# RWKV-7 trunk on one core: the chunk inverse from 16-blocks, its product in 64x64 tiles, and two stages in program order

## The chip, the core and the metric

The kernel runs on one core of a Trainium2 chip. A core has TensorE (PE, which writes its products to PSUM), VectorE (DVE), ScalarE (ACT) and GpSimd (POOL), and SyncE (SP), which issues most transfers. Each engine runs its own list of instructions from front to back; semaphores tie the lists together. The metric is the device time of one execution in microseconds (us).

## The reference, cut to what matters

Two decoder layers on 512 tokens of width 1024. The change lies in the first, the RWKV-7 time mixing. For each of 16 heads of width 64 a state matrix S runs through the tokens:

```python
def step(S, inp):
    r_t, d_t, k_t, v_t, a_t, b_t = inp
    sa = jnp.einsum('bhij,bhj->bhi', S, a_t)
    S = (S * d_t[:, :, None, :] + sa[..., None] * b_t[:, :, None, :]
         + v_t[..., None] * k_t[:, :, None, :])
    return S, jnp.einsum('bhij,bhj->bhi', S, r_t)
...
y = ((y - mean) * lax.rsqrt(var + GN_EPS)).reshape(B, T, D)      # per head
bonus = jnp.sum(r_h * k_h * r_k.astype(f32), axis=-1, keepdims=True) * v_h
y = y + bonus.reshape(B, T, D)
return (y * g.astype(f32)).astype(x.dtype) @ w_o
```

Behind it come a convolutional FFN, the attention layer and a second FFN; nothing in them is changed.

## The kernel before

The tokens are cut into 8 chunks of 64 (`CH`). Within a chunk the recurrence becomes matrix algebra: per chunk and head a unit triangular 64x64 matrix has to be inverted; after that the chunk needs only products, and a scan over the 8 chunks carries the state. Heads stand in pairs: 8 pairs `q`, and `h` = 0 or 1 for the upper or lower 64 partitions.

The stage goes from about 196 to 423 us of the span. First part, the operands:
- `v_steps` makes V with 16 groups of 12 products of 512 columns (L745). For two groups it takes a block of weights, which ACT rounds to fp32r (`whi`, L102) and POOL subtracts (`wlo`, L107); in the first eight groups ACT and DVE also make the mixed input `xv` (L337, L342, L719, L720).
- `inverse(hf)` handles four chunks, `E0` or `E1`. `mats` multiplies `bk` with `ar` into 64x64 matrices (L953) and masks them into `E` (L955). The two 32x32 diagonal blocks of each are then laid out with one matrix per partition by DVE transposes (L964) and inverted by substitution: 30 columns `k`, for each a product into `tmp` (L978) and a sum (L979) over (31-k)*k numbers. Transposes bring the result back (L987, L991); the block off the diagonal takes two rounds of 32x32 products (`corner`, L1001) and copies by ACT (L1004).
- `attn_mats` makes per chunk the matrices `G` (L912) and `R` (L920). Each is masked either by DVE straight from PSUM (L890) or by an ACT copy (L887) and a POOL product (L888).
- `with_inverse` (L933) multiplies `G` of a chunk with its inverse; ACT copies the result out (L936).

Second part, `scan`, per chunk: products of `G` with the state (L1103) and of `ar` with the state (L1106); DVE and ACT copy the solution out (L1110, L1111); a product with `bT` (L1120) gives the new state, which DVE puts together (`sn` L1123, `SV` L1125); `R` ends the output `py` (L1129); `bkT` (L1034) makes the next chunk's `bT`. `norm` of a chunk is called one chunk later: eight small steps on DVE and ACT (L1044 to L1053), after which PE transposes `yc` and `bv` (L1062) and ACT copies them (L1063). From chunk 4 on two output gates follow per chunk (`gate`: ACT L1163, POOL L1164 and L1165, PE L1168, then `gated`: DVE L1180, L1181, ACT L142, DVE L143). In the chunks 0 to 3 `fill` places steps of the second inverse and of `attn_mats` between these.

What sets the order: a string `ORDER` says how the program emits the operands' steps (`V`, `N`, `M`, `s`: one step of V, of `mats`, of `attn_mats`, of the inverse), the tables `FM` and `FS` how many steps `fill` emits. That is only the order of emission. The program is built with a scheduler that models each engine and moves instructions against each other; only a stretch under `tc.manual_schedule()` stays as emitted. Before, that is the projections' stage (string `START`) alone; the operands and the scan are moved by the scheduler.

Of the kernel before, what the change touches and what calls it, by code (L numbers as in the profile page):

```python
# [35 lines left out]
KS = (99, 26)  # L36
# [11 lines left out]
MV = 2  # L48
VLO = 'PPPPDDDD'
VB = (4, 4)  # L50
ORDER = 'VVNVNVNVNVsssMVsMVsMVMVMMsssssVMMsssssVMMsssssVMMnsssssVMMnsssssnMMssssssVsVsnMVVnssVsMb'
SCB = 6
AORD = 'qsqqqsqsqspsqoqspvpsqvspvsvpqspoqsvpvspvqsvovpsopvppvpossovvvpovvppo'
PTB = 2
# [12 lines left out]
CC = {}  # L67
# [9 lines left out]
class Net:  # L77
# [272 lines left out]
    def rwkv(self, after_pool):  # L350
        nc, tc, d, par = self.nc, self.tc, self.d, self.par
# [5 lines left out]
        gm = pA.tile([128, 2, T], F32, name="gm")  # L357
# [3 lines left out]
        cst = pA.tile([128, CC["gmask"]], F32, name="cst2")  # L361
        tri, mask = (cst[:, CC[k]:CC[k] + 128] for k in ("tri", "mask"))
# [9 lines left out]
        eng = {"D": nc.vector, "P": nc.gpsimd}  # L372
# [17 lines left out]
        for k in FIRST:  # L390
            q = nc.scalar if k.isupper() else nc.sync
# [308 lines left out]
        bs, box = self.ps(), {}  # L700
# [50 lines left out]
        v = v_steps()  # L751
        box["m"] = lambda: t2("m")
        sums = lambda: None
        for q in range(8):
# [6 lines left out]
            for n in range(4):  # L761
                ns = slice(n * 128, n * 128 + 128)
# [38 lines left out]
        sp0 = tc.alloc_tile_pool(name="s0", bufs=1, reuse_waits="tile")  # L801
        aa0 = tc.alloc_tile_pool(name="aa0", bufs=1, reuse_waits="tile")
        mixv = tc.alloc_tile_pool(name="rX", bufs=1, reuse_waits="tile")
        box["m"] = lambda: mixv.tile([128, T], F32, name="m", tag="m", bufs=MV)
        self.ar, self.bk, self.fdec, self.amask, self.gmask = ar, bk, fdec, mask, tri

        nc.sync.dma_start(tri, d["cst"][:, CC["gmask"]:CC["gmask"] + 128])

        def bonus():
# [7 lines left out]
            for h in range(2):  # L817
# [3 lines left out]
        E0, n0, s0 = self.inverse(0, sp0, sp0)  # L821
# [1 line left out]
        A0, m0 = self.attn_mats(0, aa0, "A")  # L823
        run = {"M": lambda: next(m0, None), "V": lambda: next(v, None), "N": lambda: next(n0, None), "n": lambda: next(n1, None),
               "s": lambda: s0(1), "S": lambda: s1(1), "b": bonus}
        for k in ORDER:
            run[k]()
        for g in (v, m0, n0, n1):
            for _ in g:
                pass  # L830
        s0(99)
        mixv.release()
        w24.release()
        A1, m1 = self.attn_mats(1, self.mixp, "mx")
        sp = tc.alloc_tile_pool(name="sc", bufs=1, side="right", reuse_waits="tile")
        rest = self.scan(sp, (A0, A1), (E0, E1), m1, s1, aa0, sp0, gm)
        for p in (sp, self.mixp, pB):
            p.release()
        if self.dbg:
# [85 lines left out]

    def with_inverse(self, G, E, n0):

        nc = self.nc
        P = [self.ps().rearrange("a (q x) -> a q x", q=8) for _ in range(2)]
        for q in range(8):  # L930
            for h in range(2):
                hs = slice(64 * h, 64 * h + 64)
                nc.tensor.matmul(P[h][:, q, :], G[hs, q, :], E[hs, n0 + q, :], start=True, stop=True, skip_group_check=True)  # L933
        A = G.rearrange("a q x -> a (q x)").rearrange("a (h q x) -> a h q x", h=2, q=8)
        for h in range(2):
            nc.scalar.copy(A[:, h], P[h])  # L936
        return A

    def inverse(self, hf, pool, sp):

        nc = self.nc
        box = {}
        E = pool.tile([128, 32, CH], F32, name=f"E{hf}", tag=f"E{hf}", bufs=1)

        def mats():
            for c4 in range(4):
                p = self.ps()
                for q in range(8):  # L950
                    for h in range(2):
                        hs = slice(64 * h, 64 * h + 64)
                        nc.tensor.matmul(p[hs, CH * q:CH * q + CH], self.bk[hs, q, 4 * hf + c4, 0, :], self.ar[hs, q, 0, 4 * hf + c4, :],  # L953
                                         start=True, stop=True, skip_group_check=True)
# [4 lines left out]
        def tin(qd):
            if qd == 0:  # L960
                box["P"] = sp.tile([128, 32, 32], F32, name="P", tag="P")
            dd = qd % 2
            rows = slice(32 * qd, 32 * qd + 32)
            nc.vector.transpose(box["P"][rows], E[rows, :, 32 * dd:32 * dd + 32].rearrange("a n t -> a t n"))  # L964

        def nin(h):
            if h == 0:
                box["NT"] = sp.tile([128, 32, 32], F32, name="NT", tag="NT")
            nc.vector.transpose(box["NT"][64 * h + 32:64 * h + 64], E[64 * h:64 * h + 32, :, 32:64])

        def sub(k):
            n, P = 31 - k, box["P"]
            eng = nc.gpsimd if k > KS[hf] else nc.vector
            tmp = sp.tile([128, 256], F32, name="tmp", tag="tmp")
            tv = tmp[:, 0:n * k].rearrange("a (t s) -> a t s", s=k)
            a0 = P[:, k, 0:k].unsqueeze(1).broadcast_to([128, n, k])
            a1 = P[:, k + 1:32, k:k + 1].broadcast_to([128, n, k])
            eng.tensor_tensor(tv, a0, a1, ALU.mult)  # L978
            eng.tensor_tensor(P[:, k + 1:32, 0:k], P[:, k + 1:32, 0:k], tv, ALU.add)  # L979

        def ones():
            nc.gpsimd.memset(box["P"].rearrange("a t s -> a (t s)")[:, 0:1024:33], 1.0)

        def tout(i):
            P = box["P"]
            if i == 0:
                nc.vector.transpose(E[:, :, 32:64].rearrange("a n t -> a t n"), P)  # L987
            else:
                rows = slice(64 * (i - 1), 64 * (i - 1) + 32)
                nc.scalar.copy(E[rows, :, 0:32], E[rows, :, 32:64])  # L990
                nc.vector.transpose(box["NT"][rows].rearrange("a n s -> a s n"), P[rows].rearrange("a t s -> a s t"))  # L991

        def corner(st, g):
            NT = box["NT"]
            p = self.ps()
            for j in range(16):
                n = 16 * g + j
                for h in range(2):
                    o = p[64 * h:64 * h + 32, 32 * j:32 * j + 32]
                    rw = slice(64 * h + 32 * (1 - st), 64 * h + 32 * (1 - st) + 32)  # L1000
                    nc.tensor.matmul(o, NT[rw, n, :], E[rw, n, 32:64], start=True, stop=True, skip_group_check=True)  # L1001
            for h in range(2):
                rw = slice(64 * h, 64 * h + 32)
                nc.scalar.copy(E[rw, 16 * g:16 * g + 16, 32:64], p[rw].rearrange("a (n t) -> a n t", t=32))  # L1004

        todo = [(tin, (i,)) for i in range(4)] + [(sub, (k,)) for k in range(30, 0, -1)] + [(ones, ())]
        todo += [(nin, (i,)) for i in range(2)] + [(tout, (i,)) for i in range(3)] + [(corner, (st, g)) for st in range(2) for g in range(2)]
# [551 lines left out]
```

## Time and profile before

| | us |
|---|---|
| median of 3 runs | 1438.5 (1436.83 to 1443.36) |
| the profiled execution | 1444.57 |
| its span, first to last instruction | 1442.8 |
| PE busy in the span | 1339.2 (93%) |
| DVE, ACT, POOL busy | 965.2, 664.6, 601.1 |
| mean granted TensorE clock | 0.958 |

Lines of the profile name an engine, a line of the kernel, the operation, the tile written and the tiles read. An `x` gives a count. A PE product of fp32 operands shows as two records, one of fp32r operands as one. `[4.67 <-ACT G L936]` is the time that the engine stood idle before, and what it waited for. [...]

### The profile page before, as it was taken

The numbers are of one execution on the slowest core, as the hardware profiler recorded it, in microseconds if no ns is written. First come the engines' busy times: TensorE is split into PE (matmuls) and PEld (weight loads), VectorE is DVE, ScalarE is ACT, GpSimd is POOL, SyncE is SP. The second block draws the span as 40 slices with busy tenths as digits, with TensorE's granted clock in tenths as the row PEclk, the third lists the DMA queues.
The fourth block names the chain that finished last, engine by engine and source line by source line (L and its number), as shares of the span: only waits on it lengthen the run. The fifth ranks groups of instructions, "written<-read, shape, count | busy, mean of one in ns | idle before, by whom it ended". The sixth has DMA issues, their size and how long they took to land.

```text
span 1442.8 us, 24180 instructions
## 1 busy us (share of the span) xinstructions
PE 1339.2 (93%) x9848; PEld 1119.7 (78%) x9848; DVE 965.2 (67%) x1368; ACT 664.6 (46%) x1210; POOL 601.1 (42%) x405
## 2 busy tenths in 40 slices
PE   4889988769879999999999999999999999999996
PEld 4757767668779888888888899867897888888886
DVE  7787789686688677777632167887667877773214
ACT  6436542325456444444322357866544444343222
POOL 6774563426543533333321444523534334332244
PEclk9899999869899999999999999999999999999998
DMA  5121121000245142332323343412323233323333
GB/s 195 37 77 62 60 60 35 13 9 19 75 140 164 70 132 88 102 100 90 98 83 103 98 152 96 144 45 73 103 74 131 75 104 100 102 86 95 91 97 123
DMA packets 43584, 129.94 MB, mean 90 GB/s; under 512 B 4561, under 2 KB 12497, under 8 KB 43473
## 3 DMA queue, kind: packets, MB, share of 16 engines
q1 hardware_dynamic: 41072, 126.11, 28.1%
q10 hardware_dynamic: 2400, 2.29, 0.5%
q8 instruction: 77, 1.26, 0.4%
q14 instruction: 35, 0.28, 0.1%
HBM read 124.19 MB, written 2.10 MB: 88 GB/s over the span
## 4 chain that ended last, share of the span: by engine, by line
PE 62%; DVE 4%; ACT 1%; issue 1%; POOL 0%; DMA 0%; DVEq 0%; ACTq 0%; POOLq 0%
PE ps L124 19%; PE ps L126 19%; PE ps L125 19%; PE ps L1397 2%; PE ps L1361 1%; PE ps L1360 1%; DVE h L198 1%; DVE X L210 1%; DVE wlo L107 1%; PE ps L1387 1%; ACT h L197 1%; DVE acc L173 0%; POOL wlo L107 0%; DVE yy L209 0%; PE ps L154 0%
## 5 line engine op out<-in xcount | busy, mean ns | idle before, releaser
L107 POOL TENSOR_TENSOR wlo<-raw,whi 128x1024 fp32r<-128x1024 f32 (+1 forms) x134 | 323.6, 2417 | 365.0 <-ACT whi L102 302.3
L102 ACT CAST whi<-raw 128x1024 fp32r<-128x1024 f32 (+1 forms) x215 | 219.5, 1025 | 319.1 <-PE ps L125 240.1
L125 PE MATMUL ps<-h,whi 128*128 128x512 f32 (+1 forms) x984 | 358.5, 365 | 3.3 <-DVE h L198 3.1
L126 PE MATMUL ps<-h,wlo 128*128 128x512 f32 (+1 forms) x984 | 358.2, 365 | 2.8 <-DVE wlo L107 1.8
L124 PE MATMUL ps<-h,whi 128*128 128x512 f32 (+1 forms) x984 | 358.9, 367 | 0.0
L107 DVE TENSOR_TENSOR wlo<-raw,whi 128x1024 fp32r<-128x1024 f32 (+1 forms) x81 | 108.2, 1336 | 173.7 <-ACT whi L102 173.6
L125 PEld LDWEIGHTS ps<-h,whi 128*128 128x128 f32 x984 | 187.9, 191 | 34.5 <-DVE h L198 4.0
L126 PEld LDWEIGHTS ps<-h,wlo 128*128 128x128 f32 x984 | 187.7, 191 | 34.6 <-DVE wlo L107 2.7
L124 PEld LDWEIGHTS ps<-h,whi 128*128 128x128 f32 x984 | 186.8, 191 | 33.9 <-issue 2.7
L303 POOL TENSOR_TENSOR cs<-cs 128x512 f32<-128x512 f32 x44 | 57.7, 1312 | 243.2 <-DVE cs L295 213.6
L125 PE MATMUL ps<-g,whi 128*128 128x512 f32 (+1 forms) x440 | 153.8, 349 | 0.0
L124 PE MATMUL ps<-g,whi 128*128 128x512 f32 (+1 forms) x440 | 153.4, 349 | 0.0
L126 PE MATMUL ps<-g,wlo 128*128 128x512 f32 (+1 forms) x440 | 153.4, 349 | 0.0
L143 DVE TENSOR_TENSOR g<-cs,g 128x512 fp32r<-128x512 f32 x44 | 93.6, 2126 | 41.5 <-ACT g L142 41.5
L173 DVE TENSOR_TENSOR acc<-acc,sq 128x256 f32<-128x256 f32 x56 | 49.0, 889 | 72.6 <-ACT sq L172 72.3
L125 PEld LDWEIGHTS ps<-g,whi 128*128 128x128 f32 x440 | 82.6, 188 | 12.2
L126 PEld LDWEIGHTS ps<-g,wlo 128*128 128x128 f32 x440 | 82.6, 188 | 12.2
L124 PEld LDWEIGHTS ps<-g,whi 128*128 128x128 f32 x440 | 82.6, 188 | 12.1
L302 ACT ACTIVATE cs<-cs 128x512 f32<-128x512 f32 x44 | 27.8, 632 | 120.7 <-DVE cs L295 120.7
L292 DVE TENSOR_TENSOR rp<-ps,rsx 128x512 f32<-128x512 f32 x88 | 59.7, 686 | 31.3 <-PE ps L126 31.2
L293 ACT ACTIVATE cs<-rp,par 128x512 f32<-128x512 f32 x88 | 70.3, 811 | 16.1 <-DVE g L143 8.6
L294 DVE SCALAR_TENSOR_TENSOR cs<-rp,par,cs 128x511 f32<-128x511 f32 x88 | 74.0, 846 | 1.9 <-ACT cs L293 1.9
(303 smaller groups left out, 2490.5 us busy)
## 6 DMA issues: line engine op xcount, KB each, us to landing
raw<-w_up SPq DMA_DIRECT2D x88, 512.0 KB, 3.6
raw<-w_down SPq DMA_DIRECT2D x40, 512.0 KB, 3.5
raw<-w_or SPq DMA_DIRECT2D x16, 512.0 KB, 3.9
raw<-w_q SPq DMA_DIRECT2D x16, 512.0 KB, 3.7
raw<-w_oa SPq DMA_DIRECT2D x16, 512.0 KB, 3.6
raw<-w_down SPq DMA_DIRECT2D x20, 384.0 KB, 3.2
raw<-w_k SPq DMA_DIRECT2D x8, 512.0 KB, 3.5
raw<-w_r SPq DMA_DIRECT2D x8, 512.0 KB, 3.5
```

Of the source, the lines that this page charges most:

```text
L102: (nc.vector.tensor_copy if lo and lo[-1] == "v" else nc.scalar.copy)(hi, raw)
L107: (nc.gpsimd if lo[0] == "P" else nc.vector).tensor_tensor(wl, raw, hi.bitcast(F32), ALU.subtract)
L124: mm(p, hi, ah, start=first, stop=False, skip_group_check=True)
L125: mm(p, hi, al, start=False, stop=False, skip_group_check=True)
L126: mm(p, lo, ah, start=False, stop=last, skip_group_check=True)
L143: self.nc.vector.tensor_tensor(lo, src, hi.bitcast(F32), ALU.subtract)
L173: (eng or nc.vector).tensor_tensor(acc[:, o:o + n], acc[:, o:o + n], sq, ALU.add)
L292: nc.vector.tensor_tensor(r, p, rsx, ALU.mult)
L293: nc.scalar.activation(c, r, AF.Identity, bias=par[:, cb:cb + 1], scale=par[:, cw + 88:cw + 89])
L294: nc.vector.scalar_tensor_tensor(c[:, 1:], r[:, :T - 1], par[:, cw + 44:cw + 45], c[:, 1:], ALU.mult, ALU.add)
L303: nc.gpsimd.tensor_tensor(cs[:, 0], cs[:, 0], cs[:, 1], ALU.mult)
L1397: self.nc.tensor.matmul(po[64 * h:64 * h + 64, :], self.V[:, n - o, 64 * kvh:64 * kvh + 64], pt[:, o].rearrange("a i q -> a (i q)"), start ...
```

## The change

Three things change, all in the RWKV stage.

1. The inverse. `mats` now puts both 32x32 diagonal blocks into columns 32 to 63 of `E`, by three products with 32 rows of output per head instead of one with 64 (L963). One transpose of all 128 partitions lays them out (L973). The substitution runs only within the 16x16 diagonal blocks, both at once: 14 columns, 2*(15-k)*k numbers each, all on DVE (L982, L983). The 16x16 blocks off the diagonal come from PE: `below`, once 128 and once 256 products of 32x32 weights with 16 columns (L1005), with an ACT step (`low`, L1013), POOL memsets and two DVE sums (`add`, L1017) between. `corner` (L1027, L1029) has its two rounds with other operands and more ACT copies in the first (L1037, L1038).
2. `with_inverse` is written as two 64x64 products per matrix (L937) where one with 128 columns of weights stood.
3. The operands' loop over `ORDER` and the call of `scan` stand under `tc.manual_schedule()`, with new strings `ORDER` and `FS`. The code of `scan` is otherwise the same.

```diff
-FS = ((4, 4, 3), (4, 4, 3), (4, 4, 4), (4, 4, 2))
+FS = ((3, 3, 2), (3, 3, 2), (2, 2, 2), (2, 2, 0))
-ORDER = 'VVNVNVNVNVsssMVsMVsMVMVMMsssssVMMsssssVMMsssssVMMnsssssVMMnsssssnMMssssssVsVsnMVVnssVsMb'
+ORDER = 'VNVNVNVNVsssMVsssMVsssMVsssMVsssMVsssMVssMVssMVssMVssMVVMMMVnMVnMVnMVnMb'
...
-        for k in ORDER:
-            run[k]()
+        with tc.manual_schedule():
+            for k in ORDER:
+                run[k]()
...
-        rest = self.scan(sp, (A0, A1), (E0, E1), m1, s1, aa0, sp0, gm)
+        with tc.manual_schedule():
+            rest = self.scan(sp, (A0, A1), (E0, E1), m1, s1, aa0, sp0, gm)
...
-                hs = slice(64 * h, 64 * h + 64)
-                nc.tensor.matmul(P[h][:, q, :], G[hs, q, :], E[hs, n0 + q, :], start=True, stop=True, skip_group_check=True)
+                for i in range(2):
+                    hs, ms = slice(64 * h, 64 * h + 64), slice(64 * ((h + i) % 2), 64 * ((h + i) % 2) + 64)
+                    nc.tensor.matmul(P[h][ms, q, :], G[hs, q, ms], E[hs, n0 + q, :], start=True, stop=True, skip_group_check=True)
...
+                    for i, (r, t, o) in enumerate(((0, 32, 0), (0, 0, 32), (1, 0, 0))):
+                        n = 64 if r else 32
+                        for h in range(2):
+                            hs = slice(64 * h, 64 * h + 64)
+                            nc.tensor.matmul(p[Q[2 * h + r], CH * q + o:CH * q + o + n], self.bk[hs, q, c, 0, 32 * r:32 * r + 32], self.ar[hs, q, 0, c, t:t + n],
+                                             start=True, stop=True, skip_group_check=True)
...
+            nc.vector.transpose(box["P"], D.rearrange("a n t -> a t n"))
+            nc.gpsimd.memset(box["P"][:, 16:32, 0:16], 0.0)
...
         def sub(k):
+            n, B = 15 - k, box["B"]
+            tmp = sp.tile([128, 112], F32, name="tmp", tag="tmp")
+            tv = tmp[:, 0:2 * n * k].rearrange("a (b t s) -> a b t s", b=2, s=k)
+            a0 = B[:, :, k, 0:k].unsqueeze(2).broadcast_to([128, 2, n, k])
+            a1 = B[:, :, k + 1:16, k:k + 1].broadcast_to([128, 2, n, k])
+            nc.vector.tensor_tensor(tv, a0, a1, ALU.mult)
+            nc.vector.tensor_tensor(B[:, :, k + 1:16, 0:k], B[:, :, k + 1:16, 0:k], tv, ALU.add)
...
+        def below(st):
+            NT, O = box["NT"], box["P"]
+            for i in range(2 if st else 1):
+                p = self.ps()
+                for n in range(32):
+                    for r in Q:
+                        x, y = ((E[r, n, 32:64], NT[r, n, 0:16]), (O[r, n, :], E[r, n, 48:64]), (E[r, n, 32:64], O[r, n, 0:16]))[st + i]
+                        nc.tensor.matmul(p[r, 16 * n:16 * n + 16], x, y, start=True, stop=True, skip_group_check=True)
...
+        def low():
+            O = box["P"]
+            nc.gpsimd.memset(O[:, :, 16:32], 0.0)
+            nc.scalar.activation(O[:, :, 0:16], box["p", 0], AF.Copy, scale=self.low)
+        def add():
+            for i, x in enumerate((E[:, :, 48:64], box["NT"][:, :, 0:16])):
+                nc.vector.tensor_tensor(x, x, box["p", 1 + i], ALU.add)
...
+        todo = [(tin, ())] + [(sub, (k,)) for k in range(14, 0, -1)] + [(ones, ()), (tout, (0,)), (below, (0,)), (tout, (1,)), (low, ()), (below, (1,)), (add, ())]
+        todo += [(corner, (st, g)) for st in range(2) for g in range(2)]
```

ScalarE's list in the operands, around the first `G` and `R`, before. `whi` are V's weights in blocks, `G0` and `R0` the matrices of the first chunks, `X` is where V goes after its first half.

```order
L719 CAST xv_1537<-m_1823 128x512
L102 CAST whi_1763<-raw_1761 128x1024
L887 COPY G0_1516<-ps_1706 128x512
L102 CAST whi_1852<-raw_1850 128x1024
L887 COPY R0_1520<-ps_1787 128x512
L887 COPY R0_1520<-ps_1788 128x512
L748 COPY X_61<-ps_1544 128x512
```

ScalarE at the same place now:

```order
L719 CAST xv_1535<-m_1792 128x512
L890 COPY G0_1516<-ps_1818 128x512
L102 CAST whi_1839<-raw_1837 128x1024
L337 ACTIVATE m_1843<-X_61,omu_78 128x512
L719 CAST xv_1536<-m_1843 128x512
L337 ACTIVATE m_1887<-X_61,omu_78 128x512
L719 CAST xv_1537<-m_1887 128x512
L890 COPY R0_1520<-ps_1913 128x512
L102 CAST whi_1951<-raw_1949 128x1024
```

Counting V's groups from 0: before, the mixed inputs and the weights of all of the groups 0 to 7 (the last are `xv_1537` and `whi_1763`) stood ahead of the copy of the first `G0`, and `whi_1852` is already of the second half. Now the weights of the groups 4 and 5 (`whi_1839`) and the mixed inputs from `xv_1536` on stand behind that copy, and the weights of the groups 6 and 7 (`whi_1951`) behind the copy of `R0`.

VectorE's list in the scan, chunk 5, before. `ps_4018` and `ps_4019` belong to chunk 5, `ps_4020` is `py` of chunk 5.

```order
L1123 TENSOR_TENSOR sn_4085<-ps_4018,fdec_77 128x256
L1125 TENSOR_TENSOR SV_4010<-sn_4085,Sf_4013 64x256 x2
L1123 TENSOR_TENSOR sn_4097<-ps_4019,fdec_77 128x256
L1125 TENSOR_TENSOR SV_4010<-sn_4097,Sf_4013 64x256 x2
L1044 TENSOR_REDUCE st_4327<-ps_4020 128x8
```

VectorE in chunk 5 now; `ps_5055` and `ps_5056` belong to chunk 5, `ps_4831` is `py` of chunk 4.

```order
L1157 TENSOR_TENSOR sn_5138<-ps_5055,fdec_77 128x256
L1159 TENSOR_TENSOR SV_5047<-sn_5138,Sf_5050 64x256 x2
L1157 TENSOR_TENSOR sn_5150<-ps_5056,fdec_77 128x256
L1159 TENSOR_TENSOR SV_5047<-sn_5150,Sf_5050 64x256 x2
L1078 TENSOR_REDUCE st_5207<-ps_4831 128x8
```

Before, the norm that follows the state of a chunk is the norm of that chunk, one chunk ahead of its call; now it is that of the chunk before. On PE the transposes of that norm stand behind `bkT` and ahead of the next chunk's first product in both.

ScalarE in the same chunk, around the two gates, before:

```order
L1163 CAST ghi<-graw 128x256
L1051 ACTIVATE st<-st,eps 128x8
L1170 COPY g_4192<-ps 128x256
L1163 CAST ghi<-graw 128x256
L1170 COPY g_4212<-ps 128x256
L142 CAST z<-t 128x256 x2
L1111 COPY SV<-ps 64x256 x2
```

ScalarE there now:

```order
L1197 CAST ghi<-graw 128x256
L1204 COPY g_5245<-ps 128x256
L142 CAST z<-t 128x256
L1197 CAST ghi<-graw 128x256
L1204 COPY g_5265<-ps 128x256
L142 CAST z<-t 128x256
L1145 COPY SV<-ps 64x256 x2
```

The cast of the second gate's weights stood ahead of the first `z`; now it stands behind it.

## Rows read from the trace of the kernel before

**Rows 1.** Windows: start:end, length, busy us (count) per engine, PEclk, DMA share, GB/s

```profile
195.70:292.20 96.50, 80.21 (x1270) 65.70 (x1271) 77.64 (x106) 30.04 (x50) 38.31 (x35) 0.85 0.10 29
292.20:369.20 77.00, 59.05 (x1688) 54.96 (x1688) 55.98 (x111) 33.61 (x66) 35.75 (x40) 0.83 0.10 24
369.20:406.10 36.90, 33.89 (x658) 30.59 (x658) 25.53 (x54) 16.08 (x38) 16.47 (x23) 0.85 0.32 97
406.10:423.10 17.00, 9.40 (x125) 7.88 (x125) 13.21 (x23) 10.68 (x23) 7.10 (x7) 0.84 0.28 93
240.00:270.00 30.00, 18.46 (x378) 16.51 (x379) 25.70 (x45) 5.70 (x8) 7.51 (x6) 0.77 0.01 1
```

**Rows 2.** Groups by line, VectorE, 195.7 to 423.1: busy us, mean ns | idle before

```profile
L979 DVE TENSOR_TENSOR P<-P,tmp 128x130 f32<-128x130 f32 (+14 forms) x56 | 27.2, 486 | 1.8
L978 DVE TENSOR_TENSOR tmp<-P 128x130 f32<-128x130 f32 (+14 forms) x56 | 23.9, 426 | 3.3 <-POOL P L979 1.5
...
L720 DVE TENSOR_TENSOR xv<-m,xv 128x512 fp32r<-128x512 f32 x4 | 5.0, 1255 | 0.7 <-ACT xv L719 0.7
...
L987 DVE STREAM_TRANSPOSE E<-P 128x1024 f32<-128x1024 f32 x2 | 3.8, 1899 | 0.2
...
L342 DVE SCALAR_TENSOR_TENSOR m<-X,par,m 128x511 f32<-128x511 f32 x3 | 2.2, 743 | 0.8 <-ACT m L337 0.8
```

**Rows 3.** Timeline of TensorE, products of the operands: start us, length us, records

```profile
205.57 1.15 PE L953 MATMUL ps<-ar,bk 64*64 64x64 f32 x32
...
206.98 0.39 PE L745 MATMUL ps<-wlo,xv 128*128 128x512 f32 x1
207.22 0.62 PE L745 MATMUL ps<-whi,xv 128*128 128x512 f32 x2
...
279.24 1.20 PE L1001 MATMUL ps<-E,NT 32*32 32x32 f32 x64
...
325.49 2.00 PE L933 MATMUL ps<-E,G 64*128 64x64 f32 x32
...
328.41 1.10 PE L920 MATMUL ps<-ar,bk 64*64 64x64 f32 x62
```

**Rows 4.** Groups by line, ScalarE, 195.7 to 423.1

```profile
L102 ACT CAST whi<-raw 128x1024 fp32r<-128x1024 f32 x9 | 9.3, 1041 | 9.8 <-PE ps L745 9.8
...
L887 ACT COPY G<-ps 128x512 f32<-128x512 f32 x10 | 5.9, 590 | 18.9 <-PE ps L912 18.8
...
L1163 ACT CAST ghi<-graw 128x256 fp32r<-128x256 f32 x8 | 3.2, 409 | 2.9 <-DMA graw<-g 2.9
...
L337 ACT ACTIVATE m<-X,omu 128x512 f32<-128x512 f32 x3 | 2.1, 717 | 4.2 <-DVE xv L720 4.2
L719 ACT CAST xv<-m 128x512 fp32r<-128x512 f32 x3 | 1.9, 617 | 0.3 <-DVE m L342 0.2
```

**Rows 5.** Groups by line, GpSimd, 195.7 to 423.1

```profile
L107 POOL TENSOR_TENSOR wlo<-raw,whi 128x1024 fp32r<-128x1024 f32 x8 | 19.5, 2447 | 22.1 <-issue 13.4 <-ACT whi L102 8.7
...
L888 POOL TENSOR_TENSOR G<-G,cst 128x512 f32<-128x512 f32 x10 | 13.0, 1305 | 34.5 <-ACT G L887 34.4
...
L1164 POOL TENSOR_TENSOR glo<-graw,ghi 128x128 fp32r<-128x128 f32 x8 | 4.1, 514 | 4.2 <-ACT ghi L1163 2.4 <-issue 1.3
```

**Rows 6.** Timeline of VectorE, state and norm of one chunk

```profile
332.63 0.42 DVE L1123 TENSOR_TENSOR sn<-ps,fdec 128x256 f32<-128x256 f32 x1
333.09 0.87 DVE L1125 TENSOR_TENSOR SV<-sn,Sf 64x256 f32<-64x256 f32 x2
333.99 0.69 DVE L1044 TENSOR_REDUCE st<-ps 128x8 f32<-128x512 f32 x1
...
337.73 0.69 DVE L1053 TENSOR_TENSOR yc<-yc,st 128x512 f32<-128x512 f32 x1
```

**Rows 7.** Timeline of TensorE, first products of two chunks of the scan

```profile
369.24 0.69 PE L1103 MATMUL ps<-SV,G 128*64 128x64 f32 x4 [4.67 <-ACT G L936]
...
406.08 1.15 PE L1103 MATMUL ps<-SV,G 128*64 128x64 f32 x32
```

More of the change, by code (lines that the diff above doesn't have):

```diff
@@ L805, in rwkv @@
         self.ar, self.bk, self.fdec, self.amask, self.gmask = ar, bk, fdec, mask, tri
+        self.low = cst[:, CC["lo"]:CC["lo"] + 1]
         nc.sync.dma_start(tri, d["cst"][:, CC["gmask"]:CC["gmask"] + 128])
@@ L825, in rwkv @@
                "s": lambda: s0(1), "S": lambda: s1(1), "b": bonus}
-        for k in ORDER:
-            run[k]()
[L828 to L831, printed above, removed]
+        with tc.manual_schedule():
+            for k in ORDER:
+                run[k]()
+            for g in (v, m0, n0, n1):
+                for _ in g:
+                    pass
+            s0(99)
         mixv.release()
@@ L945, in inverse @@
         E = pool.tile([128, 32, CH], F32, name=f"E{hf}", tag=f"E{hf}", bufs=1)
+        D = E[:, :, 32:64]
+        Q = [slice(32 * i, 32 * i + 32) for i in range(4)]
         def mats():
             for c4 in range(4):
-                p = self.ps()
+                p, c = self.ps(), 4 * hf + c4
                 for q in range(8):
[L951 to L954, printed above, removed]
+                    for i, (r, t, o) in enumerate(((0, 32, 0), (0, 0, 32), (1, 0, 0))):
[4 more added lines that the diff above has]
+                                             start=True, stop=True, skip_group_check=True)
                 nc.vector.tensor_tensor(E[:, 8 * c4:8 * c4 + 8, :], p.rearrange("a (q t) -> a q t", q=8),
@@ L957, in mats @@
                 yield
[L959 to L969, printed above, removed]
@@ L971, in sub, with tin @@
-        def sub(k):
[L972 to L979, printed above, removed]
+        def tin():
+            F = box["F"] = sp.tile([128, 2, 528], F32, name="P", tag="P")
+            box["P"] = F.rearrange("a b x -> a (b x)")[:, 0:1024].rearrange("a (t s) -> a t s", s=32)
+            box["B"] = F[:, :, 0:512].rearrange("a b (t s) -> a b t s", s=32)
+            nc.vector.transpose(box["P"], D.rearrange("a n t -> a t n"))
+            nc.gpsimd.memset(box["P"][:, 16:32, 0:16], 0.0)
@@ L981, in ones @@
         def ones():
             nc.gpsimd.memset(box["P"].rearrange("a t s -> a (t s)")[:, 0:1024:33], 1.0)
+            box["NT"] = sp.tile([128, 32, 32], F32, name="NT", tag="NT")
         def tout(i):
             P = box["P"]
-            if i == 0:
-                nc.vector.transpose(E[:, :, 32:64].rearrange("a n t -> a t n"), P)
-            else:
-                rows = slice(64 * (i - 1), 64 * (i - 1) + 32)
-                nc.scalar.copy(E[rows, :, 0:32], E[rows, :, 32:64])
-                nc.vector.transpose(box["NT"][rows].rearrange("a n s -> a s n"), P[rows].rearrange("a t s -> a s t"))
+            if i:
+                nc.vector.transpose(D.rearrange("a n t -> a t n"), P)
+            else:
+                nc.vector.transpose(box["NT"].rearrange("a n s -> a s n"), P.rearrange("a t s -> a s t"))
@@ new lines, in below @@
+        def below(st):
[6 more added lines that the diff above has]
+                        nc.tensor.matmul(p[r, 16 * n:16 * n + 16], x, y, start=True, stop=True, skip_group_check=True)
+                pv = p.rearrange("a (n t) -> a n t", n=32)
+                box["p", st + i] = pv
@@ L998, in corner @@
                 for h in range(2):
-                    o = p[64 * h:64 * h + 32, 32 * j:32 * j + 32]
-                    rw = slice(64 * h + 32 * (1 - st), 64 * h + 32 * (1 - st) + 32)
-                    nc.tensor.matmul(o, NT[rw, n, :], E[rw, n, 32:64], start=True, stop=True, skip_group_check=True)
-            for h in range(2):
[L1003 to L1007, printed above, removed]
+                    a, b = Q[2 * h], Q[2 * h + 1]
+                    if st:
+                        nc.tensor.matmul(p[a, 32 * j:32 * j + 32], NT[b, n, :], E[b, n, 32:64], start=True, stop=True, skip_group_check=True)
+                    else:
+                        nc.tensor.matmul(p[b, 32 * j:32 * j + 32], E[a, n, 0:32], NT[a, n, :], start=True, stop=True, skip_group_check=True)
+            ns = slice(16 * g, 16 * g + 16)
+            for h in range(2):
+                a, b = Q[2 * h], Q[2 * h + 1]
+                pv = p[a if st else b].rearrange("a (n t) -> a n t", t=32)
+                if st:
+                    nc.scalar.copy(E[a, ns, 32:64], pv)
+                else:
+                    nc.scalar.copy(NT[b, ns], pv)
+                    nc.scalar.copy(E[a, ns, 0:32], E[a, ns, 32:64])
+        todo = [(tin, ())] + [(sub, (k,)) for k in range(14, 0, -1)] + [(ones, ()), (tout, (0,)), (below, (0,)), (tout, (1,)), (low, ()), (below, (1,)), (add, ())]
+        todo += [(corner, (st, g)) for st in range(2) for g in range(2)]
         def run(n):
@@ L1475, in _constants @@
     t = np.arange(64)[None]
-    cst[:, CC["mask"]:CC["mask"] + 64] = -1.0 * (s < t)
+    cst[:, CC["mask"]:CC["mask"] + 32] = -1.0 * (s < 32)
+    cst[:, CC["mask"] + 32:CC["mask"] + 64] = -1.0 * (s % 32 < t[:, 0:32])
     cst[:, CC["mask"] + 64:CC["mask"] + 128] = s <= t
```

## The prediction

> **What bounds the kernel now.** I read the windows first. From the end of the run the kernel is bound by TensorE and unchanged: behind the scan the order of all later work stays. So only 195.7 to 423.1 us is open, and I cut it at the first products of chunks 0, 4 and 7: A, the operands, 96.5 us; B, chunks 0 to 3, 77.0; C, chunks 4 to 6, 36.9; D, 17.0 to the steady output products [rows 1]. In A PE is busy 80.2 us, in B 59.1, so 34 us are idle; in C only 3. In 240 to 270 VectorE is busy 25.7 of 30 us and PE 18.5: there the substitution holds the stage [rows 1]. By the groups it is 56 products and 56 sums, 51 us [rows 2]. Next came the timelines: they give the price of each small product (spacing of starts or length over count; one fp32 product is two records), and the order of both kernels tells who stands behind whom.
>
> **The change part by part.** First the substitution. 28 instructions per inverse instead of 60, over fewer numbers, and 6 transposes instead of 18, at about 1.9 us: some 50 us less of VectorE's busy time [rows 2]. None of it counts by itself; it counts as far as PE's 34 idle us go away, which is the first rival.
>
> Second, PE's own work [rows 3]. `with_inverse`: 128 products of 2.00/16 = 0.126 us were 16.1; 256 of 64x64 at L920's 0.035 are 9.1, so -7.0. `mats`: 128 products of 0.072 were 9.2; 384 of 0.035 are 13.4, so +4 (zero to 5). `below`: 768 products that the kernel did not have. L920's and L1001's rows give 0.035 and 0.037, 28 us; if four tiles of 32 rows overlap by two more, half of it, 14. I take 0.025, 19.2 us, half in A and half in B. PE gains +16 (5 to 25) in all.
>
> Third, the operands as emitted, term A. PE's work there: 192 products of V at 0.24 (206.98 to 207.22) are 45.9; `G` eight times and `R` four times 1.1, 13.2; `mats` 13.4; `below` 9.6; `corner` and the transposes by PE about 8: 90. What waits, counted along the lists: a group of V in the first half now needs, behind the copy of `G0` (0.59), the weights' cast (1.04), the mixed input by L337 (0.72), L342 (0.74), L719 (0.62) and L720 (0.7 to 1.26) [rows 2, 4]. That is 4.7 to 5.0 us in a row on two engines, begun only when PE has ended `G` (1.1), ahead of 2.8 us of products. Groups 4 to 7 so take about 8.5, 6.8, 8.3 and 3.4 us, 27, where their PE work is 15: 12 us of wait. In the second half there is no mixed input, but the weights of the last four loads stand behind a copy of `G` or `R`: copy 0.59, cast 1.04, beside it POOL's mask 1.3, then the rounding's rest `wlo` 2.45 on POOL [rows 4, 5]. Less the PE work beside it, these waits are 4.8, 4.4, 6.7 and 2.8, 19 us. With the first mixed input (3.8) A comes to 90 + 12 + 19 + 4 = 125 instead of 96.5: **+28.5**. Bounds: if half the waits lie beside other work, +14; if PE also runs its first products after each wait as slowly as after the idle 4.67 us, where 4 records took 0.69 against 32 in 1.15 [rows 7], +34. Before, the scheduler had put all of these casts ahead of the masks, which is why such waits are small in A's 16 idle us.
>
> Fourth, the scan as emitted. PE's order there is the same as before. VectorE's is not: the norm of a chunk now runs behind the state of the next chunk, while PE's transposes of that norm stand, as before, ahead of the following chunk's first product. So PE, and with it the whole chain of states, waits for the norm. From the start of L1044 to the end of L1053 it is 337.73 + 0.69 - 333.99 = 4.4 us [rows 6]. Before, this lay beside the next chunk's products.
>
> Term B: PE's 59.1, with half of the `below` (9.6) and of what `with_inverse` gives back (3.5), is 65; three norms with their hand-overs, 3 x 4.7 = 14; and in chunk 2 the second transpose (1.90) behind copy and mask of an `R` (0.59 and 1.3), 4: 83 instead of 77, **+6**. If half of the norms is covered by `fill`'s steps and the transpose too, 72 to 75, -2; with 7 us of low clock on top, +13. The granted clock in B is 0.83 already [rows 1].
>
> Term C, per chunk: L1137, L1140 and L937 with 1.1 each, 3.3; L1154 to 4.4; two halves of the state, 0.42 + 0.87 each, to 7.0; norm to 11.4; transposes to 12.5; ACT's copy 0.59 and the gate's cast 0.41, POOL's two differences at 0.51, to 14.5; PE's four products 0.6, to 15.1. The second gate's cast stands now behind the first `z`: two steps of ACT at 0.41, POOL 1.0, PE 0.6, to 17.5 [rows 3 to 6]. Some ten hand-overs at an estimated 0.1 make it 18.5. Then the first 64 records of a chunk at the lower clock, which at twice the 0.034 of the row of 406.08 is 2 more: 20.4. Three times, 61 instead of 36.9: **+24**. Bounds: without the slow start and with the cast covered 18, without cover for anything else 27.
>
> Term D: the last chunk's gates in a row, with `wlo` of 2.45 us between on POOL, **+3** (-2 to 5).
>
> [...] In the rows two forms write both row halves into one PSUM bank: L953, 72 ns a product, and L1001, 37; L920, with a bank for each, takes 35 [rows 3]. [...]
>
> [...] L920's 62 records in 1.10 us are 18 ns from start to start [rows 3]. [...]
>
> Sum: 28.5 + 6 + 24 + 3 = 61.5. PE's +16 is inside A and B, and less than nothing of it in C. On the profiled execution of 1444.57 this gives 1506; the median of the runs is 6 lower, 1438.5 + 61.5 = **1500 us**.
>
> **The rivals.** *Only the scan's order costs.* The casts and mixed inputs are ready because ACT, busy 30 of A's 96.5 us, runs ahead; the copies that it waits behind come early enough. Against it: each copy needs PE's products of the same step. Then A is +0, B +6, C +24, D +2: 32, or 1470.
>
> *Faster.* The idle of A and B was the substitution's, and it goes; norms and gates are covered as before. Place: VectorE in 222 to 311 us. Price: -34 idle, +16 PE, -18: 1421. It decides as soon as PE doesn't stand before V's groups nor before the transposes of the norm. For it speak the 25.7 of 30 us in 240 to 270; against it that the norm's place in the two lists leaves no cover.
>
> *`below` serialises.* Four row tiles write one bank: 768 products at 0.074 (two records of L1001's 0.037 a product one after the other) are 57 us, not 19: +38, 1538. For it speaks L953, against it L1001.
>
> *No change.* The relief by the substitution (-34) meets PE's +16 and waits of 18 in the scan: 1438.
>
> **How the numbers follow.** Forecast 0.56, with its own range 1475 to 1525 from the bounds of A to D; only the scan 0.24; faster 0.09; serial `below` 0.06; no change 0.05. About 0.5%, 7 us, is what a measurement of this kernel can tell from no change. Faster by more 0.09, within 0.05, slower 0.56 + 0.24 + 0.06 = 0.86. The range 1450 to 1532 leaves out faster, no change and most of the serial case, 0.2.
>
> **What would show it.** Right: PE idle ahead of V's groups 4 to 7 and of the last four `wlo`, released by ACT, VectorE and POOL; chunk 0's first product near 321 us; PE waiting 4 to 5 us per chunk at the transposes (L1096) for VectorE's `yc` (L1087); chunks 4 to 6 at 18 to 20 us apiece; `below` (L1005) at 18 to 37 ns a product; substitution near 15 us in all. Wrong: a scan step of 12 us, or PE busy through A, with VectorE's relief turned into an earlier scan; or `below` at 70 ns and more.

## The result, and the profile after

The changed kernel takes 1562.4 us (median of 4 runs, 1557.5 to 1573.6) where the kernel before took 1440.9 on the same chip (a fourth run added to the three of the table): a ratio of 1.0846, with a 95% interval of 1.0768 to 1.0923. Slower, as forecast, but by 121 us instead of 61, and outside the range that ended at 1532.

The profiled execution took 1573.6 us, the longest of the four; its span is 1571.8 (before 1442.8). Cut at the same products of TensorE as [rows 1], the windows of the kernel after are, with the same columns:

```profile
196.50:347.10 150.60, 105.32 (x2536) 82.59 (x2532) 33.58 (x55) 32.47 (x56) 33.41 (x27) 0.82 0.07 20
347.10:457.30 110.20, 71.71 (x2585) 66.85 (x2585) 50.06 (x88) 32.95 (x62) 33.27 (x38) 0.69 0.06 15
457.30:522.40 65.10, 40.62 (x754) 30.09 (x754) 27.83 (x60) 21.62 (x48) 16.72 (x26) 0.70 0.08 20
```

A went from 96.5 to 150.6 us, B from 77.0 to 110.2, C from 36.9 to 65.1; from the last chunk's first product to the end it is 1036.7 before and 1049.4 now (D). The differences are 54.1 + 33.2 + 28.2 + 12.7 = 128 us, 7 more than the medians are apart, since this execution was the longest. VectorE, which held the stage before, is nearly empty in A: 33.6 us busy instead of 77.6. PEclk, the share of TensorE's full clock that was granted, fell from 0.83 and 0.85 to 0.69 and 0.70 in B and C.

The records of TensorE and of its clock, laid over each other, give a finer account. "Half" is busy time at a granted clock of 0.5; products of V of 512 columns (L745) start 0.43 us apart there (197.07 and 197.50), 1.2 columns a ns, which is the "1.2 GHz" of a forecast below. Half of that time is taken as lost, as an upper estimate: eight records of transposes (L1096) last 1.94 us at 0.5 and 1.06 at 1.0 in this trace, and the 32 records of L1137 1.98 us at 0.5 where [rows 7] has 1.15 at the end of a busy stretch. Smaller products lose less, so that the true loss may be nearer a third: L923's records start 27.0 ns apart at 0.5 and 15.0 at 1.0, those of `below` 13.3 and 8.4.

| us | length | idle | busy | of it half | change: idle | lost to the clock | other work |
|---|---|---|---|---|---|---|---|
| A before, after | 96.5, 150.6 | 16.3, 45.3 | 80.2, 105.3 | 19.7, 44.7 | +29.0 | +12.5 | +12.6 |
| B before, after | 77.0, 110.2 | 17.9, 38.5 | 59.1, 71.7 | 17.9, 42.6 | +20.5 | +12.3 | +0.3 |
| C before, after | 36.9, 65.1 | 3.0, 24.5 | 33.9, 40.6 | 9.3, 25.3 | +21.5 | +8.0 | -1.3 |

So 71 us are idle time, at most 33 us the clock, and 12 us other work (23 if the clock cost a third of its time and not half).

What TensorE waited for, in A (us in all, times, longest; "issue" is a wait that no semaphore explains):

```profile
PE ps L745 <- ACT xv L719: 15.8, 5, 5.5
PE ps L1005 <- issue: 9.1, 4, 2.6
PE ps L745 <- POOL wlo L107: 7.5, 4, 2.2
PE ps L745 <- ACT whi L102: 6.8, 3, 4.6
PE ps L963 <- issue: 1.9, 1, 1.9
PE ps L923 <- issue: 1.5, 1, 1.5
PE ps L1068 <- issue: 1.4, 1, 1.4
```

V's groups wait 30.1 us for casts and mixed input, and `below` (L1005) 9.1 us for nothing that a semaphore shows. In B:

```profile
PE ps L1096 <- DVE yc L1087: 20.3, 3, 10.7
PE ps L1005 <- issue: 8.9, 5, 1.8
PE ps L1005 <- POOL P L1012: 2.3, 1, 2.3
PE ps L1137 <- issue: 1.8, 1, 1.8
```

and in C:

```profile
PE ps L1096 <- DVE yc L1087: 15.6, 3, 5.9
PE ps L1202 <- ACT ghi L1197: 8.1, 6, 1.7
```

The norm's wait stands ahead of the transposes as forecast. One step of C on VectorE and TensorE, the norm of chunk 4 and what it holds:

```profile
464.75 0.69 DVE L1078 TENSOR_REDUCE st<-ps 128x8 f32<-128x512 f32 x1
...
468.43 0.69 DVE L1087 TENSOR_TENSOR yc<-yc,st 128x512 f32<-128x512 f32 x1
```

```profile
469.26 1.08 PE L1096 MATMUL ps<-io,yc 128*128 128x128 f32 x4 [4.83 <-DVE yc L1087]
470.14 1.06 PE L1096 MATMUL ps<-io,bv 128*128 128x128 f32 x4
472.18 1.91 PE L1202 MATMUL ps<-gmp,ghi 128*128 128x512 f32 x3 [0.98 <-ACT ghi L1197]
...
476.24 1.22 PE L1202 MATMUL ps<-gmp,ghi 128*128 128x512 f32 x2 [1.72 <-ACT ghi L1197]
...
478.79 1.73 PE L1137 MATMUL ps<-SV,G 128*64 128x64 f32 x32
```

The norm takes 4.4 us, as in [rows 6], and what stands behind it runs at the clock that fell in the wait, 0.5 from 466.4 to 480.1 us: the next chunk's first product starts 9.5 us after the transposes.

The stops that no semaphore explains look like this, in the second inverse's `below`:

```profile
405.20 1.90 PE L1005 MATMUL ps<-E,P 32*32 32x16 f32 x127 [2.31 <-POOL P L1012]
408.90 1.90 PE L1005 MATMUL ps<-E,P 32*32 32x16 f32 x128 [1.80 <-issue]
412.35 0.18 PE L1005 MATMUL ps<-E,P 32*32 32x16 f32 x1 [1.56 <-issue]
412.36 1.90 PE L1005 MATMUL ps<-P,E 32*32 32x16 f32 x127
416.08 1.90 PE L1005 MATMUL ps<-P,E 32*32 32x16 f32 x128 [1.82 <-issue]
419.81 0.18 PE L1005 MATMUL ps<-P,E 32*32 32x16 f32 x1 [1.83 <-issue]
```

Here TensorE stops after every 128 records, which with their weight loads are 256 instructions; in the two rounds of A 229 and 237 records ran ahead of the first stop (from 261.48 and 282.95). In 404 to 421 the transfers are five loads of instructions and nothing else:

```profile
GB/s 0 0 0 0 0 39 0 0 0 0 0 0 0 39 0 0 0 0 0 0 0 0 39 0 0 0 0 0 0 0 0 39 0 0 0 0 0 0 0 39
...
q8 instruction: 5, 0.08, 2.1%
```

Each load is 16 KB, so 64 bytes for each of 256 instructions; they start 3.4 to 3.8 us apart (406.3, 409.9, 413.4, 417.2, 420.9). Over the whole span this queue carries 95 loads, before 77. The waits named "issue" are 26.1 us in A to C; in the kernel before they were 3.0.

### The profile page after: what moved, and what is told of

It is laid out like the page before. It is cut to its first block, busy times and chain, and to the rows that moved or that the text cites. A ratio compares the mean times of both kernels' runs of the same rounds, so it can differ in the third digit from the quotient of the medians.

```text
span 1571.8 us, 28734 instructions
## 1 busy us (share of the span) xinstructions
PE 1385.6 (88%) x12152; PEld 1146.5 (73%) x12152; DVE 914.7 (58%) x1304; ACT 669.8 (43%) x1216; POOL 597.6 (38%) x401
## 4 chain that ended last, share of the span: by engine, by line
PE 57%; DVE 3%; ACT 1%; issue 1%; DMA 0%; POOL 0%; DVEq 0%; ACTq 0%; POOLq 0%
PE ps L124 17%; PE ps L126 17%; PE ps L125 17%; PE ps L1431 1%; PE ps L1395 1%; PE ps L1394 1%; DVE h L198 1%; DVE X L210 1%; DVE wlo L107 1%; PE ps L1421 1%; ACT h L197 0%; DMA raw<-w_up 0%; DVE acc L173 0%; POOL wlo L107 0%; DVE yy L209 0%
## 5 line engine op out<-in xcount | busy, mean ns | idle before, releaser
L124 PEld LDWEIGHTS ps<-g,whi 128*128 128x128 f32 x440 | 82.6, 188 | 12.3
L745 PE MATMUL ps<-whi,xv 128*128 128x512 f32 x128 | 57.0, 515 | 23.2 <-ACT xv L719 15.8
L293 ACT ACTIVATE cs<-rp,par 128x512 f32<-128x512 f32 x88 | 70.3, 812 | 16.3 <-DVE g L143 8.6
```

The lines of the kernel that those rows point to most:

```text
L124: mm(p, hi, ah, start=first, stop=False, skip_group_check=True)
L293: nc.scalar.activation(c, r, AF.Identity, bias=par[:, cb:cb + 1], scale=par[:, cw + 88:cw + 89])
L745: nc.tensor.matmul(P[n], x[:, ns], w, start=c == 0 and i == 0, stop=c == NB - 1 and i == 2, skip_group_check=True)
```

## The experiments

Theory 1: the emitted order costs the time. Theory 2, the rival: the small products cost it, by their number and the low clock. Their first four runs put back one piece of the order each.

**Operands and scan left to the scheduler** (all arithmetic of the change, its strings `ORDER` and `FS`):

```diff
-        with tc.manual_schedule():
-            for k in ORDER:
-                run[k]()
+        for k in ORDER:
+            run[k]()
...
-        with tc.manual_schedule():
-            rest = self.scan(sp, (A0, A1), (E0, E1), m1, s1, aa0, sp0, gm)
+        rest = self.scan(sp, (A0, A1), (E0, E1), m1, s1, aa0, sp0, gm)
```

> The changed kernel with its new inverse, its 64x64 products and its strings ORDER and FS, but operands and scan left to the scheduler as before. Theory 1 (the order costs): nearly all of the 121 us goes, 1440 to 1460, since only the added products of TensorE stay. Theory 2 (the small products cost by themselves, 1536 records of `below` at 24 ns with stops of 2 us every 128 records, and the low clock that they bring): about 1480 to 1500.

Measured 1460.9 beside 1446.8 for the kernel before (ratio 1.0095, 1.0047 to 1.0144). Theory 1 for most of it. But the arithmetic alone (with its strings; the old strings were not tried with it) makes the kernel 0.9% slower, though the substitution is shorter. B is 90.0 us instead of 77.0 and C 36.2, and of the waits in 185 to 436 one stands far ahead of the rest (L1003 is `below` here):

```profile
PE ps L1003 <- issue: 19.3, 10, 3.6
```

In A the shorter substitution did reach TensorE. In the kernel before it stood in VectorE's list ahead of two masks that TensorE waited for:

```profile
PE ps L912 <- DVE R L890: 8.7, 1, 8.7
...
PE ps L912 <- DVE G L890: 5.4, 1, 5.4
```

These 14.1 us are gone here, but 14.1 us of stops that no semaphore explains have come in A, and A is 102.9 us where it was 96.5.

**Only the scan as emitted** (the first half of the diff above):

> As the changed kernel, but only the scan stays as emitted; the operands are left to the scheduler. Theory 1: B, C and D keep their +33, +28 and +13 us, A its 96 us: about 1505 to 1515, and TensorE still waits some 36 us ahead of the transposes L1096. Theory 2: the operands' +55 stay for the most part too, 1545 or more.

1522.7 (1.0511, 1.0473 to 1.0549), 8 us above theory 1's end, far from theory 2's: A 110 from 185 us on (162 in the changed kernel, 107 before), B 106.7, C 66.1, and 1054.4 to the end.

**Only the operands as emitted** (the second half):

> As the changed kernel, but only the operands stay as emitted; the scan is left to the scheduler. Theory 1: A keeps its 151 us, chunks 4 to 6 go back to 12 us each: about 1495 to 1505. Theory 2: TensorE's low clock and the stops of `below` in the chunks 0 to 3 stay, 1520 or more.

1505.5 (1.0412, 1.0387 to 1.0436), at theory 1's end: A 158 from 185 us on, B 88.4, C 35.0. The parts add up. Arithmetic 0.95%, the scan's order 5.11 - 0.95 = 4.16%, the operands' order 4.12 - 0.95 = 3.17%: together 8.3%, and the change measured 8.5%.

**The norm's first part one chunk earlier**, the order else as in the change:

```diff
+            nrm = norm(*pend.pop()) if pend else None
+            if nrm:
+                next(nrm)
             fill(c, 0)
...
-            if pend:
-                for _ in norm(*pend.pop()):
-                    pass
+            if nrm:
+                for _ in nrm:
+                    pass
```

> The changed kernel, with one thing moved: VectorE's and ScalarE's part of the norm of a chunk is emitted right behind the copies of the next chunk's solution, ahead of its state, and TensorE's transposes stay where they are. Theory 1 (the norm's place holds the scan): most of the 36 us ahead of L1096 go and the clock rises with it, 1505 to 1530. Rival (the state's sums are late instead, or gates and clock set the step): 1545 to 1565.

1537.6 (1.0623, 1.0588 to 1.0659), 2.1% less than the changed kernel, between the two forecasts. The 35.9 us ahead of the transposes are 3.2 (rows of B and C):

```profile
PE ps L1205 <- ACT ghi L1200: 8.8, 6, 1.7
...
PE ps L1096 <- DVE yc L1087: 3.2, 3, 2.0
```

In this profile B and C are 90.7 and 50.7 us, 34 less together, and the clock there is 0.81 and 0.79. A step of C is still 16.9 us, not 12.3. So the norm's place is the cause of about half of what the scan's order costs.

**Also the gates of chunks 5 to 7 earlier**, ahead of the products with `bT`:

```diff
+            if c > 4:
+                for b in (2 * (c - 4), 2 * (c - 4) + 1):
+                    self.gate(b)
             fill(c, 0)
...
-            if c >= 4:
-                for b in (2 * (c - 4), 2 * (c - 4) + 1):
+            if c == 4:
+                for b in (0, 1):
                     self.gate(b)
```

> The kernel of e4_norm_early, with the two output gates of the chunks 5 to 7 also emitted early, ahead of the products with bT. If the gates' casts behind the transposes' copies hold the rest of a step (TensorE waits 9 us for `ghi` in six gates): chunks 4 to 6 go from 16.9 to 12 or 13 us each, 1515 to 1528. If the state's chain or the clock holds the rest: within 5 us of e4_norm_early.

1537.3 (1.0651, 1.0620 to 1.0683): no gain. The wait only changed its place. The gate's cast now stands on ScalarE behind the norm's square root, and TensorE's products of the gate, ahead of the state's, wait for it longer:

```profile
PE ps L1208 <- ACT ghi L1203: 15.5, 6, 4.9
```

Neither hand-written place is good; the scheduler's steps of C take 12 us (35.0 in all with only the operands as emitted). What is left of C's loss with the norm early, 50.7 against 35.0, no run here takes away.

**V's casts one group ahead**, the order else as in the change:

```diff
-                    if c % 2 == 0 and c + h > 0:
-                        W = load(h, c // 2)
                     whi, wlo = W[c % 2]
-                    if h == 0 and c >= VA:
+                    if h == 0 and c >= VA and c not in done:
                         mix(c)
+                    if c % 2 and c + h < NB:
+                        W = load(h + (c + 1) // NB, (c + 1) % NB // 2)
+                    if h == 0 and VA <= c + 1 < NB:
+                        mix(c + 1)
+                        done.add(c + 1)
```

> The changed kernel, where V's weights and mixed input for the next group are emitted ahead of a group's products instead of behind them, so that ScalarE's casts stand ahead of the next copies of `G` and `R`; nothing else is moved. Theory 1 (the casts' place holds the operands): the 31 us that TensorE waits for xv, whi and wlo go for the most part and the clock rises, the first product of chunk 0 comes 15 to 35 us earlier, 1527 to 1547. Rival (the supply of instructions and the clock hold A by themselves): less than 8 us earlier, 1554 or more.

1530.1 (1.0592, 1.0566 to 1.0618). Chunk 0's first product comes at 308.5 us instead of 347.1, and of V's 30 us of waits (L749 here) 4.4 are left, in 185 to 308.5:

```profile
PE ps L1009 <- issue: 8.0, 4, 2.5
...
PE ps L749 <- ACT xv L719: 2.8, 2, 2.0
```

A became 38 us shorter for 26 us of waits; the clock in the 96 us ahead of that product rose from 0.82 to 0.86. So the place of the casts behind the copies of `G` and `R` is the cause of 38 of A's 54 us. The other 16 are, by the account of the table, mostly TensorE's added work (12).

The other runs ask why the arithmetic by itself costs time. Theory F, by loads 3.4 to 3.8 us apart as above: TensorE is supplied with instructions at no more than 256 per 3.5 us.

**`below` twice** in the kernel with the scheduler's order:

```diff
-                        nc.tensor.matmul(p[r, 16 * n:16 * n + 16], x, y, start=True, stop=True, skip_group_check=True)
+                        for _ in range(2):
+                            nc.tensor.matmul(p[r, 16 * n:16 * n + 16], x, y, start=True, stop=True, skip_group_check=True)
```

> The kernel of e1_free (all arithmetic of the change, order left to the scheduler), with each product of `below` issued twice into the same place, so 1536 more records and 3072 more instructions on TensorE. In its trace TensorE stops for 1.5 to 3.6 us in `below` after every 128 records, beside a load of 16 KB of instructions; between the stops a record takes 8 to 13 ns. Theory F (the supply of instructions sets the pace, one load of 256 instructions per 3.5 us): +35 to +42 us on e1_free. Rival (the products or their bank in PSUM set it, 8 to 13 ns a record): +13 to +20.

1505.7 (1.0433, 1.0398 to 1.0468), so 44.8 us more in the medians and 49 by the ratios (the kernel before ran 4.6 us faster on this chip), for 12 more loads (107): 3.7 to 4.1 us each. That is above theory F's range and more than twice the rival's. The stops grew from 19.3 to

```profile
PE ps L1004 <- issue: 38.7, 22, 3.8
```

This also speaks against a shared PSUM bank. Between the stops of the changed kernel a record starts 8.4 ns after the last at a granted clock of 1.0 and 13.3 at 0.5, with four row tiles in one bank; with the records doubled it is 9.4 and 13.7. The 1536 added records at that pace are 13 to 21 us.

**`with_inverse` alone changed, in the kernel before:**

```diff
-                hs = slice(64 * h, 64 * h + 64)
-                nc.tensor.matmul(P[h][:, q, :], G[hs, q, :], E[hs, n0 + q, :], start=True, stop=True, skip_group_check=True)
+                for i in range(2):
+                    hs, ms = slice(64 * h, 64 * h + 64), slice(64 * ((h + i) % 2), 64 * ((h + i) % 2) + 64)
+                    nc.tensor.matmul(P[h][ms, q, :], G[hs, q, ms], E[hs, n0 + q, :], start=True, stop=True, skip_group_check=True)
```

> The kernel before with `with_inverse` alone written as two 64x64 products. By the products' price (128 of 0.126 us against 256 of 0.035): -7, 1432 to 1442 on a chip where before takes 1440 to 1447. Theory F: 512 more instructions are two loads, the gain is at most 4 us, or none where a load is late.

1439.2 beside 1442.2 (0.9994, 0.9970 to 1.0019): no difference. It has two loads more, 79.

**`below` in eight pieces in the operands, with V and `G` between:**

```diff
-FS = ((3, 3, 2), (3, 3, 2), (2, 2, 2), (2, 2, 0))
+FS = ((3, 3, 2), (3, 3, 2), (2, 2, 9), (2, 2, 0))
-ORDER = '...ssMVssMVssMVssMVVMMMVnMVnMVnMVnMb'
+ORDER = '...ssMVssMssVssMssVsssMVssVMMMVnMVnMVnMVnMb'
...
-(low, ()), (below, (1,)), (add, ())]
+(low, ())] + [(below, (1, j)) for j in range(8)] + [(add, ())]
```

The 9 in `FS` keeps the eight pieces of the second inverse together where its second round stood.

> The changed kernel, where the 512 products of the second round of `below` in the operands are emitted in eight pieces with groups of V and of `G` between them, in the same operands' order otherwise; the scan as it was. Theory F: the loads run while V's long products do, most of the four stops of 1.8 to 2.6 us in this round go, 6 to 12 us less than the changed kernel. Rival (the low clock or the waits on casts hold A, not the stops): no change within 4 us.

1558.8 (1.0791, 1.0753 to 1.0828). The profile's first product of chunk 0 is 6.9 us earlier and the stops of `below` in A fall from 9.1 to 6.2; but the intervals of the two ratios overlap. Inconclusive.

**The same pieces under the scheduler, spread over chunks 1 and 2 too:**

```diff
-FS = ((3, 3, 2), (3, 3, 2), (2, 2, 2), (2, 2, 0))
+FS = ((6, 6, 4), (2, 2, 2), (2, 2, 2), (3, 2, 0))
```

> All arithmetic of the change, order left to the scheduler as in e1_free, but the second round of `below` emitted in eight pieces of 64 products, with V, `G`, `R` and the scan's products between them, the second inverse's steps moved one chunk earlier in `fill`. Theory F (the supply of instructions): the stops of e1_free, 19 us in `below`, go for the most part, since the next load runs while longer products do: 1440 to 1450 where e1_free took 1461 and before 1442 to 1447. Rival (the stage holds as many loads as before, one per 3.5 us, and they bind wherever the records stand): 1455 to 1462.

1456.7 (1.0112, 1.0077 to 1.0146), no better than in one piece (1.0095). The stops in `below` fell to 12.8 us, yet at eight other lines they are 12.0 us together, where they were 7.3 at five: 24.8 in all instead of 26.6. B is 89.9 us as it was. Theory F's forecast of 1440 to 1450 failed: where the records stood did not matter here, and the loads are as many, 95, as in one piece.

**The same with the old `with_inverse`:**

> As e9_split_free, with `with_inverse` as in the kernel before: 128 products of 0.126 us in place of 256 of 0.035, 256 records (two loads of instructions) fewer. Theory F: within 3 us of e9_split_free, either way, as e6_wi was within 0.3% of the kernel before. By the products' price alone: 5 to 7 us more.

1462.2 (1.0126, 1.0090 to 1.0162): the same within the intervals, with 93 loads.

**Work in the norm's wait**, in the changed kernel:

```diff
-                for _ in norm(*pend.pop()):
+                nrm = norm(*pend.pop())
+                next(nrm)
+                p = self.ps()
+                for _ in range(16):
+                    nc.tensor.matmul(p[:, 0:128], self.ident, self.ident, start=True, stop=True, skip_group_check=True)
+                for _ in nrm:
                     pass
```

> The changed kernel with 16 products of the identity with itself (32 records, some 2 to 4 us, result unused) ahead of each chunk's transposes L1096, in the time that TensorE waits for the norm there. They add work, so no part of the scan can become shorter but by the granted clock. Theory C (the low clock after each wait costs half of the 43 us and 25 us that TensorE works at 1.2 GHz in chunks 0 to 3 and 4 to 6): 8 to 25 us less than the changed kernel, mean clock in chunks 4 to 6 above 0.8. Rival (the low clock only falls on work that nothing waits for): no change or up to 10 us more.

1554.0 (1.0798, 1.0749 to 1.0846), 8 us less in the medians, but the intervals of the two ratios overlap. In its profile B and C are shorter by 9.2 and 3.5 us with more to do, at a clock of 0.83 and 0.82 instead of 0.69 and 0.70:

```profile
345.50:446.50 101.00, 76.30 (x2680) 71.38 (x2680) 48.82 (x88) 32.76 (x62) 32.75 (x39) 0.83 0.07 17
446.50:508.10 61.60, 47.93 (x848) 38.32 (x848) 27.82 (x60) 21.42 (x48) 17.21 (x27) 0.82 0.08 21
```

The four profiles with the scan as in the change (the changed kernel, only the scan as emitted, V's casts ahead, `below` in pieces in the operands) have 103.1 to 110.2 us for B and 65.1 to 67.7 for C; both are shorter here. So in these profiles the low clock costs time, at the lower end of what was expected of it; the total does not show it clear of noise.

How much it costs stays an estimate. With only the scan as emitted and with V's casts ahead, TensorE worked in B for 37.3 and 29.3 us at a granted clock of 0.5 instead of 42.6, and was busy for 1.6 and 4.9 us less: about a third of the difference. By a third, the table's 33 us would be 22. No version was measurably faster than the kernel before.

## Why the prediction was right and wrong

- **Substitution: right that it wins nothing by itself.** Its 56 instructions take 22.2 us instead of 51, though not the 15 that I had named (groups by line, 196.5 to 522.4):

```profile
L982 DVE TENSOR_TENSOR tmp<-P 128x28 f32<-128x28 f32 (+6 forms) x28 | 11.4, 409 | 0.7
L983 DVE TENSOR_TENSOR P<-P,tmp 128x28 f32<-128x28 f32 (+6 forms) x28 | 10.8, 385 | 1.0
```

  VectorE had 44 us less to do in A. With the order left to the scheduler this ended TensorE's 14.1 us of waits for its masks, and the stops took as much; with the emitted order the waits for casts came on top. The rival "faster" failed at the point it named: TensorE stands ahead of V's groups and of the transposes.
- **Price of `below`: wrong, the first step that failed.** I took 0.025 us a product, 19.2 in all. The four stretches of L1005 last 5.4 + 12.3 + 5.0 + 14.8 = 37.5 us, 24 ns a record. Not that the products are slow: between the stops their records start 8.4 ns apart at a granted clock of 1.0 and 13.3 at 0.5, closer than in any row of [rows 3]. What I lacked is the supply of instructions. In the kernel before, the rows of such records in [rows 3] are 32 to 64 long, with 3.0 us of "issue" waits in A to C, so they could not show it. Here a stop took 1.6 to 2.6 us, where the 128 records of a block run in 1.1 to 1.9.
- **Products of `mats` and `with_inverse`: no term of weight.** Work other than idle and clock rose by 12 to 23 us over A to C, where I had +16.
- **Waits in the operands: right in mechanism and size,** wrong in what they bring. Forecast 12 + 19 + 4 = 35 us, measured 30.1, and removed by emitting the casts ahead. A's clock stood in my sum only as the upper bound of +34. It cost 8 to 12.5 us more than before, and the stops are 13.9, so A became +54 instead of +28.5.
- **The norm in the scan: right.** 35.9 us ahead of L1096 in B and C, for the reason given. In B I had three waits of 4.7 us; the first was 10.7, because VectorE had the second inverse's substitution and a mask ahead of it in its list:

```profile
368.14 1.32 DVE L983 TENSOR_TENSOR P<-P,tmp 128x88 f32<-128x88 f32 x1
...
374.78 0.87 DVE L1159 TENSOR_TENSOR SV<-sn,Sf 64x256 f32<-64x256 f32 x2
375.69 0.69 DVE L893 TENSOR_TENSOR R<-ps,cst 128x512 f32<-128x512 f32 x1
376.29 0.19 DVE L982 TENSOR_TENSOR tmp<-P 128x28 f32<-128x28 f32 x1
376.52 0.57 DVE L983 TENSOR_TENSOR P<-P,tmp 128x28 f32<-128x28 f32 x1
377.00 0.68 DVE L1078 TENSOR_REDUCE st<-ps 128x8 f32<-128x512 f32 x1
```

  With stops of 12.2 us and up to 12.3 us of clock, neither of which had a term in B, it is +33 and not +6.
- **C: right.** +28.2 for +24 forecast, 21.7 us a chunk for 20.4, in the order of steps written down; its sum alone had a term for the clock, 2 us a chunk, where the table has at most 2.7. Its 0.1 us a hand-over was an estimate from no row; from the end of the norm to the transposes the trace has 0.14 (469.12 to 469.26).
- **D: mis-sized,** +12.7 for +3. It belongs to the scan's order: from the last chunk's first product to the end, the seven profiles with an emitted scan take 1041.0 to 1054.4 us, mean 1045, and the seven with the scheduler's 1031.5 to 1040.5, mean 1035. So about 10 us; its own chain was not taken apart.
- **The rivals.** "Only the scan's order costs" is refuted by the 3.2% of the operands. "`below` serialises" came near the time by its +38 but not by its mechanism: between stops a record starts 8.4 to 13.3 ns after the last, not 37. The sum failed by two costs that had no term in A and B. TensorE's stops for instructions are 26.1 us there instead of 3.0. By the estimates above its work at a granted clock of 0.5 cost 17 to 25 us more than before, where I had the clock only in the upper bounds. The first norm's longer wait and D make up most of the rest. The waits for casts and norms, on which the forecast rested, came as forecast.

## What to carry to other kernels

Before code is left in the order in which it is written, read for each hand-over what stands ahead of the producer in its own list: a cast behind a copy that waits for TensorE, or a norm behind the state it doesn't need, turns cover into a wait in every iteration. Charge such a wait twice on TensorE, once as idle time and once as low clock in what follows: here the granted clock was 0.5 for 13.7 us around and behind a wait of 4.83, and the second charge is estimated at a third to a half of the time worked at 0.5. And count instructions, not only columns: the products of `below`, 8.4 to 13.3 ns a record between stops, took 24 over their stretches, since instructions arrived at 256 per 3.4 to 3.8 us.

## What was not expected of the hardware

TensorE's instructions arrived at about 256 per 3.4 to 3.8 us when small products stood in a row, about 14 ns an instruction or 28 ns a record with its weight load; between the stops records started 8.4 ns apart at a granted clock of 1.0 and 13.3 at 0.5. Instruction loads counted as 77, 79, 93, 95 and 107 in kernels that differ by 512 to 7680 instructions of TensorE, one for each 256. Doubling 1536 records cost 44.8 us, where the records themselves run in 13 to 21.
